# TensorE's order in the second stage written by a driver over bursts, head pairs in one burst, row sums on POOL

## The chip, the cores and the metric

The kernel runs on one core of one Trainium2 chip. The metric is the device time of one execution in microseconds; it is the time of that core. The core's engines are TensorE (PE in the profile), VectorE (DVE), ScalarE (ACT), GpSimd (POOL) and SyncE (SP); each runs its own list of instructions in the order in which the program fixes it, and they meet at semaphores.

## What is computed

One layer of an encoder for two request groups: a prompt group (one stream of 2048 frames) and a sample group (eight streams, 16 frames each, with 4096 past rows). All tensors are float32. Each frame of 1024 features goes through one combined input projection, three parallel groups of heads, and one output projection; a LayerNorm closes the layer. Cut to what matters here:

```python
def _layer(x, w_in, ..., w_out, ln_g, ln_b, hg_state, mem_k, mem_v, ...):
    hq, hf, hv, hgate, fq, fk, fv, fgate, flogf, mq, mgate = _split_in(x @ w_in)
    ...
    o_h, S = _hgrn2(hg_state, q, k, v, log_f)        # gated linear recurrence, 4 heads of 128
    o_f = _fox_prompt(fq, fk, fv, logf)              # attention with decay, 4 heads of 64
    o_m = _cross(mq, mem_k, mem_v)                   # attention to 256 memory rows, 4 heads of 64
    mix = concat(rmsnorm(o_h) * silu(hgate), o_f * silu(fgate), o_m * silu(mgate))
    return layernorm(ALPHA * x + mix @ w_out)
```

## The kernel before, in words

The first stage (up to 1006.65 us) does the input projection, the sample group's attention over its cache and the prompt's first two FoX blocks, and writes what the heads need to DRAM. Products that must keep float32 precision are made of three products of split operands (`xh*wh`, `xh*wl`, `xl*wh`).

The second stage (from 1006.65 us on) is the change's place. The prompt is cut into 16 tiles of 128 frames. For each tile `t` there are three pieces:

- `cross(t)` (from L1143): scores of four heads against the 256 memory rows, in both PSUM banks `f`; a maximum (L1158, VectorE), four exponentials (L1161, ScalarE), transposes, eight values products `h<-cPT,mvt`, a gate.
- `hgrn_tile(t)` (L679): q and k are multiplied by decays level by level (`update`, L708 to L710, VectorE), and after each level TensorE makes a few small products of 32 columns (`L<-hQ,hK`, `h<-hQ,hK`). Then `A`, the state's products, a norm (L823), four transposes (L826), the gate (L828), and `emit_mix`: a cast to `mixHh` (L675, ScalarE) and the rest `mixHl` (L676, VectorE).
- `out_tile(t)` (L1188): two halves of 24 products `o` of the mixes with `woh` and `wol`, the residual (L1207), statistics (L1208) and the LayerNorm passes L1224 and L1225 on VectorE; the tile goes out.

Beside them runs `fox(n)` (L956) for the blocks n = 2 and 3 of 512 queries. For each of two pairs of heads it loads q (`fq1`, `fq2`, two buffers each) and then, for each 128 keys, k and v; it makes the scores of both heads (two products a head, in the banks `f`), their exponentials `fP` (L1003, ScalarE, four buffers), one values product for each head, 64 columns wide, into two halves of the bank `pv` (a float32 product counts as two records), and it adds `fP` to the row sums `facc` (L976, VectorE). q and k come by DMAs that POOL issues (L962 to L965, L989, L991).

The order of the work: `run` (L1229) calls the tiles and FoX in turn by weights; `ahead` (L1237) gives their instructions priorities (`P_CROSS` and `P_HGRN` 1000, `P_FOX` 100), and a scheduler then sets the order of each engine from its own estimates. `load_w_out` (L1105) loads the output weights in eight pieces and splits each half on ScalarE (L1118) and VectorE (L1119), between the steps of tile 0. PSUM's eight banks are `f` twice, `pv`, `h` twice, `L`, and `o` twice.

Of the kernel before, what the change touches and what calls it, by code (L numbers as in the profile page):

```python
# [21 lines left out]
B_FP = 4  # L22
B_O, B_H = 2, 2
FOX_EXTRA = 5
KW, B_WR = 4, 1
FOX_END = 70
P_X = 400
P_CROSS, P_HGRN, P_FOX = [1000, 1000, 100]
# [58 lines left out]
def kernel(  # L87
# [591 lines left out]
    def hgrn_tile(t, hb, psh, psl, hstate, emit_mix, bufs):  # L679
# [10 lines left out]
        V = tl([128, 512], "hV", 1)  # L690
        G = tl([128, 4, 128], "hG", 1)
# [6 lines left out]
        yield  # L698
        L = psl()
        P = F.rearrange("p h t -> p (h t)")  # L700

        def update(b, P):
            n = 512 // (2 * b)
            Pv = P.rearrange("p (n two) -> p n two", two=2)
            q = Q[:, 0].rearrange("p h (n two b) -> p (h n) two b", two=2, b=b)[:, :, 1, :]
            k = K.rearrange("p h (n two b) -> p (h n) two b", two=2, b=b)[:, :, 0, :]
            Pn = tl([128, n], f"P{2 * b}", bufs if b > 2 else 1)
# [9 lines left out]
        yield  # L717
        slot = 2
        M = None
        for b in (2, 4, 8) if smp else (2, 4, 8, 16):  # L720
            P = update(b // 2, P)
            if slot == 4:
                M = psh()
# [6 lines left out]
            yield  # L730
        n2 = slot - 4
        T = tl([128, 768], "hT", 1).rearrange("p (h s t) -> p h s t", h=4, s=6)[:, :, 0:slot, :]
        DVE.tensor_tensor(out=T[:, :, 0:4, :], in0=L, in1=lm3[:, 0:4, :].unsqueeze(1).to_broadcast([128, 4, 4, 32]),
                          op=ALU.mult)
        DVE.tensor_tensor(out=T[:, :, 4:slot, :], in0=M[:, :, 0 : 32 * n2].rearrange("p h (s t) -> p h s t", t=32),
                          in1=lm3[:, 4:slot, :].unsqueeze(1).to_broadcast([128, 4, n2, 32]), op=ALU.mult)
        C = tl([128, 4, 32], "hC", 1)
        DVE.tensor_reduce(out=C, in_=T.rearrange("p h s t -> p h t s"), axis=AX.X, op=ALU.add)
        A = tl([128, 4, 128], "hA", 1)
        DVE.tensor_tensor(out=A.rearrange("p h (i t) -> p h i t", t=32), in0=C.unsqueeze(2).to_broadcast([128, 4, 4, 32]),  # L740
                          in1=bm3.unsqueeze(1).to_broadcast([128, 4, 4, 32]), op=ALU.mult)
        if not smp:
            P = update(16, P)
            for h in range(4):
# [4 lines left out]
            yield  # L749
            P = update(32, P)  # L750
            for h in range(4):
                mm(M[0:64, h, 64:128], K[:, h, 0:64], Q[:, 0, h, 64:128])
            ACT.copy(A[0:64, :, 64:128], M[0:64, :, 64:128])
            ACT.copy(A[0:32, :, 32:64], M[64:96, :, 64:96])
            ACT.copy(A[64:96, :, 96:128], M[96:128, :, 64:96])
            P = update(64, P)
        else:
            P = update(8, P)
        yield
# [3 lines left out]
        o = psh()  # L763
        if not smp:
            kT = tl([128, 768], "hT", 1)[:, 0:512].rearrange("p (h t) -> p h t", h=4)
            ACT.copy(kT, kp)
            S = hstate["S"]
# [11 lines left out]
            hstate["S"] = S2  # L779
            if t == 15:  # L780
                SP.dma_start(p_state, S2)
        else:
            P3 = P.rearrange("p (h b) -> p h b", b=8)
# [31 lines left out]
        yield  # L815
# [7 lines left out]
        DVE.tensor_tensor(out=on, in0=o, in1=ss.unsqueeze(2).to_broadcast([128, 4, 128]), op=ALU.mult)  # L823
        tp = psh()
# [5 lines left out]
        yield  # L830

    def sample_hgrn(stack):
# [12 lines left out]
        yield from hgrn_tile("s", hs, ptr, lambda: pp.tile([128, 512], F32, name="pj", tag="pj", bufs=B_PJ).rearrange("p (h s t) -> p h s t", h=4, s=4), {},  # L845
# [110 lines left out]
    def fox(n):  # L956
        T0 = 512 * n
        c0 = T0 if n < 2 else T0 + 128
        for pr in range(2):
            hs = slice(2 * pr, 2 * pr + 2)  # L960
            q1 = fp.tile([68, 2, 512], F32R, name="fq1", bufs=2)
            POOL.dma_start(q1[0:64], s_qq[0:64, hs, T0 : T0 + 512])  # L962
            POOL.dma_start(q1[64:68], s_m[:, n, pr])
            q2 = fp.tile([128, 2, 512], F32R, name="fq2", bufs=2)
# [3 lines left out]
            todo = []  # L968

            def values(V, st, t0, PT, first, last):  # L970
# [3 lines left out]
                if not first:  # L974
                    for hh in range(2):
                        DVE.tensor_tensor(out=acc[hh][:, t0:], in0=acc[hh][:, t0:], in1=PT[hh][:, t0:], op=ALU.add)  # L976

            for c in range(n + 1):
# [3 lines left out]
                for st in range(4):  # L982
# [10 lines left out]
                    if todo:  # L993
                        todo.pop(0)()
# [10 lines left out]
                    todo.append(lambda V=V, st=st, t0=t0, PT=PT, first=first, last=last: values(V, st, t0, PT, first, last))  # L1005
                    yield
            while todo:
                todo.pop(0)()
            yield
# [13 lines left out]
            yield  # L1023

    def fox_steps(n):
        return 2 * (4 * (n + 1) + 2)
# [24 lines left out]
    SAMPLE_STEPS = DECODE_STEPS + 9  # L1051
# [75 lines left out]
    hstate = {"S": Sp}  # L1127
# [5 lines left out]
    def psl():  # L1133
        return pb.tile([128, 4, 4, 32], F32, name="L", tag="L", bufs=1)

# [7 lines left out]
    def cross(t):  # L1143
# [7 lines left out]
        l = ob.tile([128, 4], F32, name="cl")  # L1151
        pss = [ptf().rearrange("p (c s) -> p c s", c=2) for _ in range(2)]
# [13 lines left out]
        yield  # L1166
        PT = ob.tile([128, 8, 128], F32, name="cPT", bufs=1)
        for half in range(2):
# [4 lines left out]
            ACT.copy(PT[:, half * 4 : half * 4 + 4, :], pt)  # L1173
        o = psh()[:, 0:2, :]
# [11 lines left out]
        yield  # L1186

    def out_tile(t):  # L1188
# [14 lines left out]
        for half in range(2):  # L1203
            c = slice(512 * half, 512 * half + 512)
            ps = ptile("o", B_O)
            project(ps, lambda k: lhs(0, k), lambda k: lhs(1, k), lambda k: woh[:, k, c], lambda k: wol[:, k, c])
            DVE.scalar_tensor_tensor(out=y[:, c], in0=y[:, c], scalar=ALPHA, in1=ps, op0=ALU.mult, op1=ALU.add)  # L1207
            DVE.bn_stats(bs[:, half, :], y[:, c])  # L1208
            yield
# [17 lines left out]
        yield  # L1227

    def run(*streams):  # L1229
        live = [[g, 0, n] for g, n in streams]  # L1230
        while live:
            s = min(live, key=lambda e: (e[1] + 1) / e[2])
            if next(s[0], "end") == "end":
                live.remove(s)
            s[1] += 1

    def ahead(gen, offset):  # L1237
        while True:
            with tc.high_priority(offset=offset):
                r = next(gen, "end")  # L1240
            if r == "end":
                return
            yield

    def tiles():
        wo = load_w_out()
        next(wo)
        for t in range(16):
            for gen, offset in ((cross(t), P_CROSS), (hgrn_tile(t, hb, psh, psl, hstate, emit_mix, 2), P_HGRN)):
                for _ in ahead(gen, offset):  # L1250
                    if t == 0:
                        next(wo, None)
                        next(wo, None)
                    yield
            if t == 0:
                finish(wo)
                yield from out_tile("s")
            yield from out_tile(t)

# [4 lines left out]
    run((tiles(), 16 * 14 + 3), (ahead(fox_gen, P_FOX), (sum(fox_steps(n) for n in range(4)) - EARLY_STEPS) * 100 / FOX_END))  # L1264
# [72 lines left out]
```

## Time and profile before

| | |
|---|---|
| median of three runs | 1597.71 us (1595.32 to 1601.28) |
| profiled execution, its own time | 1597.58 us |
| its span | 1595.8 us |
| first stage, second stage | 1006.65 us, 589.15 us |
| mean granted TensorE clock | 0.985 |
| TensorE, VectorE, ScalarE, POOL busy | 1512.4, 794.4, 481.7, 168.7 us |

The span reaches from the first to the last instruction; 1.8 us of the execution's time lie around it. Busy time of TensorE counts a matmul's record; records overlap by some 0.1 us, so the time that one holds the engine is read from its start to the start of the next. A granted clock of 1.00 is 2.4 GHz, 0.50 is 1.2 GHz. In the timelines `x2` counts adjacent records of one kind, and what stands in brackets is the idle time ahead and the engine and line that ended it.

### The profile page before, as it was taken

How to read it: one execution, taken by the hardware profiler on the slowest of the kernel's cores; microseconds unless marked ns; L12 is line 12 of the kernel's file. 1: busy time of each engine (PE TensorE's matmuls, PEld its weight loads, DVE VectorE, ACT ScalarE, POOL GpSimd, SP SyncE). 2: the span in 40 equal slices, each digit the busy share in tenths (PEclk: the TensorE clock that was granted, in tenths of full speed). 3: DMA queues.
4: the chain of work that ended last, by engine and by line, in shares of the span. 5: the costliest groups of instructions: out<-in, count | busy, mean ns of one | idle time of the engine just before them, and what ended most of it. 6: DMA issues, size and time to landing. Idle time of an engine off the chain costs nothing.

```text
span 1595.8 us, 29721 instructions
## 1 busy us (share of the span) xinstructions
PE 1512.4 (95%) x12119; PEld 1183.6 (74%) x12119; DVE 794.4 (50%) x1630; ACT 481.7 (30%) x1088; POOL 168.7 (11%) x219
## 2 busy tenths in 40 slices
PE   6999999999999989889899999889999999999998
PEld 6999998986986778678887876456566566667776
DVE  4522332221343245555575223477766666668776
ACT  4323322112132311121111333444344333334341
POOL 0610000000001110000010222310111111100000
PEclk9999999999999999999999999999999999999999
DMA  7645459568669864866353675963443343322231
GB/s 245 211 134 170 135 187 293 186 209 260 218 228 277 271 195 145 227 195 189 88 149 127 155 143 119 221 174 91 130 114 97 88 110 97 91 74 87 94 100 60
DMA packets 219527, 254.71 MB, mean 160 GB/s; under 512 B 40190, under 2 KB 165310, under 8 KB 219392
## 3 DMA queue, kind: packets, MB, share of 16 engines
q1 hardware_dynamic: 165984, 217.32, 43.4%
q0 software_dynamic: 53408, 35.51, 11.2%
q8 instruction: 95, 1.56, 0.4%
q14 instruction: 40, 0.33, 0.1%
HBM read 199.55 MB, written 53.12 MB: 158 GB/s over the span
## 4 chain that ended last, share of the span: by engine, by line
PE 71%; DMA 15%; DVE 6%; issue 4%; ACT 3%; SPq 1%; POOL 0%; DVEq 0%; ACTq 0%; POOLq 0%
PE pj L119 32%; PE o L119 11%; PE pv L119 6%; PE h L119 6%; PE f L119 6%; DMA wraw<-in_w_feat_dram 4%; DMA rb<-s_r 2%; PE ds L119 2%; PE dv L119 2%; DMA fP<-s_fg 2%; PE L L119 1%; PE tr L119 1%; DMA xr<-in_x_feat_dram 1%; PE h L1172 1%; DVE wlo L259 1%
## 5 line engine op out<-in xcount | busy, mean ns | idle before, releaser
L119 PE MATMUL pj<-xh,whi 128*128 128x384 f32 (+1 forms) x1056 | 360.9, 342 | 2.8 <-DVE fmx L917 2.7
L119 PE MATMUL pj<-xh,wlo 128*128 128x384 f32 (+1 forms) x1056 | 350.2, 332 | 0.2 <-DVE wlo L259 0.2
L119 PE MATMUL pj<-xl,whi 128*128 128x384 f32 (+1 forms) x1056 | 349.3, 331 | 0.0
L119 PEld LDWEIGHTS pj<-xh,whi 128*128 128x128 f32 x1056 | 201.0, 190 | 22.3 <-issue 15.1
L119 PEld LDWEIGHTS pj<-xl,whi 128*128 128x128 f32 x1056 | 200.8, 190 | 7.4 <-issue 3.6
L119 PEld LDWEIGHTS pj<-xh,wlo 128*128 128x128 f32 x1056 | 200.2, 190 | 3.8 <-issue 3.1
L304 ACT ACTIVATE e<-pj 128x384 f32<-128x384 f32 (+1 forms) x96 | 45.3, 473 | 361.9 <-PE pj L119 324.8
L917 DVE TENSOR_REDUCE fmx<-pj 128x1 f32<-128x512 f32 (+3 forms) x160 | 96.7, 609 | 76.0 <-PE pj L119 74.3
L119 PE MATMUL pj<-whi,xh 128*128 128x256 f32 (+1 forms) x408 | 122.1, 300 | 12.3 <-ACT whi L258 8.7
L259 DVE TENSOR_TENSOR wlo<-wraw,whi 128x1024 fp32r<-128x1024 f32 (+1 forms) x60 | 75.4, 1256 | 115.2 <-ACT whi L258 115.0
L976 DVE TENSOR_TENSOR facc<-facc,fP 128x512 f32<-128x512 f32 (+3 forms) x144 | 83.7, 597 | 72.9 <-ACT fP L1003 72.6
L1003 ACT ACTIVATE fP<-f 128x512 f32<-128x512 f32 (+3 forms) x144 | 73.0, 526 | 153.8 <-PE f L119 146.1
L119 PE MATMUL pj<-whi,xl 128*128 128x256 f32 (+1 forms) x408 | 116.6, 286 | 3.0 <-DVE xl L239 3.0
L119 PE MATMUL pj<-wlo,xh 128*128 128x256 f32 (+1 forms) x408 | 116.3, 285 | 0.5 <-DVE wlo L259 0.5
L119 PE MATMUL pv<-fP,fV 128*64 128x512 f32 (+3 forms) x288 | 105.3, 565 | 5.8 <-ACT fP L1003 5.5
L119 PE MATMUL f<-fq,fk 68*128 68x512 f32 (+5 forms) x320 | 101.2, 407 | 3.4 <-issue 2.0
L119 PEld LDWEIGHTS pj<-whi,xh 128*128 128x128 f32 x408 | 78.5, 193 | 28.5 <-issue 13.1
L119 PEld LDWEIGHTS f<-fq,fk 68*128 68x128 f32 (+1 forms) x320 | 54.5, 195 | 59.0 <-issue 48.6
L258 ACT CAST whi<-wraw 128x1024 fp32r<-128x1024 f32 (+1 forms) x60 | 62.9, 1048 | 101.4 <-DMA wraw<-in_w_feat_dram 95.0
L119 PE MATMUL pj<-fk1m,fq1m 66*128 66x512 f32 (+3 forms) x160 | 64.7, 406 | 23.4 <-DMA fq1m<-s_qq 13.4
L989 POOL DMA_DIRECT2D fk<-s_kk x40 | 39.9, 998 | 398.4 <-PE f L119 393.1
L119 PEld LDWEIGHTS pj<-whi,xl 128*128 128x128 f32 x408 | 78.4, 192 | 4.9 <-DVE xl L239 4.0
(313 smaller groups left out, 2459.2 us busy)
## 6 DMA issues: line engine op xcount, KB each, us to landing
kv<-in_cache_fox_k_dram SPq DMA_DIRECT2D x64, 512.0 KB
kv<-in_cache_fox_v_dram SPq DMA_DIRECT2D x64, 512.0 KB
wraw<-in_w_feat_dram SPq DMA_DIRECT2D x56, 512.0 KB
fk<-s_kk POOLq DMA_DIRECT2D x40, 256.0 KB, 4.5
xr<-in_x_feat_dram SPq DMA_DIRECT2D x34, 256.0 KB
rb<-s_r SPq DMA_DIRECT2D x32, 256.0 KB
y<-in_x_prompt_dram SPq DMA_DIRECT2D x16, 512.0 KB
out_dram<-y SPq DMA_DIRECT2D x16, 512.0 KB
```

Source lines behind the costliest of these rows:

```text
L119: PE.matmul(out, lhsT=lhsT, rhs=rhs, start=start, stop=stop)
L258: pin(ACT.copy(hi[:, r, :w], raw[:, :, :w]))
L259: pin(DVE.tensor_tensor(out=lo[:, r, :w], in0=raw[:, :, :w], in1=hi[:, r, :w].bitcast(F32), op=ALU.subtract))
L304: ACT.activation(e, ps, AF.Sigmoid)
L917: DVE.tensor_reduce(out=mx[:, hh, tt, c : c + 1], in_=ps, axis=AX.X, op=ALU.max)
L976: DVE.tensor_tensor(out=acc[hh][:, t0:], in0=acc[hh][:, t0:], in1=PT[hh][:, t0:], op=ALU.add)
L989: POOL.dma_start(k1, s_kk[64:132, hs, cs])
L1003: ACT.activation(pT[:, t0:], ps[:, t0:], AF.Exp)
L1172: PE.transpose(pt[:, j, :], Pr[:, i // 2, (i % 2) * 128 : (i % 2) * 128 + 128], ident)
```

## The change

1. **Order by a driver.** `run`, `ahead`, `tiles` and the priorities go. `hgrn_tile`, `cross`, `fox` and `out_tile` now yield ahead of each burst of TensorE's work: the tile width of the burst, its estimated duration, a delay from the end of the burst before it, and, where needed, a gate. `drive` holds five streams (even hgrn tiles, odd ones, cross, FoX, out), keeps a clock of its own, prefers a burst of the shape that stands, and takes them in the order hgrn, cross, out, FoX, or with FoX ahead of out while FoX is behind `FOX_US`. TensorE's instructions stay in the order written. `have["H"]` is set once a tile's last hgrn burst is placed.
2. **Both heads of a values product** stand in one burst, after a yield of their own; scores, values and sums of FoX are steps of their own, and `FOX_EXTRA` goes from 5 to 6 such finer steps.
3. **POOL.** The adds to `facc` move from VectorE to POOL. The second LayerNorm pass of each tile but the last becomes a scaling on ScalarE and an add of `lnb` on POOL.
4. **Buffers.** `fP` 4 to 5; `o` 2 banks to 1, and a bank `M` for hgrn's later levels; `hV`, `hG` and `P2` two buffers, `hkT` a tile of its own; `fq1` and `fq2` 2 to 1.
5. **hgrn.** The first four slots of `T` are multiplied while the later levels are made, `A` is made in `within` ahead of the last level; the state's products have a gate on the tile before.
6. **w_out** is loaded and split as a whole ahead of the driver.

```diff
-B_FP = 4
-B_O, B_H = 2, 2
-FOX_EXTRA = 5
+B_FP = 5
+B_O, B_H = 1, 2
+FOX_EXTRA = 6
-P_CROSS, P_HGRN, P_FOX = [1000, 1000, 100]
+FOX_US, FOX_BY = 100.0, 400.0
...
-        yield
+        yield 32, 0.6, 4.0, lambda: hstate["L"]
+        hstate["L"] = False
         L = psl()
...
+        yield 128, 0.45, 5.0
         tp = psh()
         for h in range(4):
             PE.transpose(tp[:, h, :], on[:, h, :], ident)
...
-            q1 = fp.tile([68, 2, 512], F32R, name="fq1", bufs=2)
+            q1 = fp.tile([68, 2, 512], F32R, name="fq1", bufs=1)
...
-            q2 = fp.tile([128, 2, 512], F32R, name="fq2", bufs=2)
+            q2 = fp.tile([128, 2, 512], F32R, name="fq2", bufs=1)
...
-                        DVE.tensor_tensor(out=acc[hh][:, t0:], in0=acc[hh][:, t0:], in1=PT[hh][:, t0:], op=ALU.add)
+                        POOL.tensor_tensor(out=acc[hh][:, t0:], in0=acc[hh][:, t0:], in1=PT[hh][:, t0:], op=ALU.add)
...
-                    if todo:
-                        todo.pop(0)()
+                    size = (512 - t0) / 512
+                    yield 128, 0.95 * size + 0.1 * (c == n), 3.0 if first else 0.3
...
-                    todo.append(lambda V=V, st=st, t0=t0, PT=PT, first=first, last=last: values(V, st, t0, PT, first, last))
-                    yield
+                    yield 64, 0.95 * size, 1.8
+                    values(V, st, t0, PT, first, last)
...
+        yield 64.5, 1.3, 3.0
         pss = [ptf().rearrange("p (c s) -> p c s", c=2) for _ in range(2)]
...
-            ps = ptile("o", B_O)
-            project(ps, lambda k: lhs(0, k), lambda k: lhs(1, k), lambda k: woh[:, k, c], lambda k: wol[:, k, c])
+            for k in range(8):
+                if k % 2 == 0:
+                    yield 128, 1.4, 0.0 if k or B_O > 1 else 1.5
+                if k == 0:
+                    ps = ptile("o", B_O)
+                mm(ps, lhs(0, k), woh[:, k, c], start=(k == 0), stop=False)
...
-            DVE.scalar_tensor_tensor(out=y, in0=y, scalar=rs[:, 0:1], in1=lnb, op0=ALU.mult, op1=ALU.add)
+            ACT.activation(y, y, AF.Copy, scale=rs[:, 0:1])
+            POOL.tensor_tensor(out=y, in0=y, in1=lnb, op=ALU.add)
...
+    def hgrn_tiles(first):
+        for t in range(first, 16, 2):
+            busy[first] = t
+            yield from hgrn_tile(t, hb, psh, psl, hstate, emit_mix, 2, psm)
+            have["H"] = t + 1
...
+    def out_ready():
+        t = need["O"]
+        return t == "s" or min(have["H"], have["C"]) > t and fox_done[0] > t // 4
...
+            can = [s for s in (h, g, x, f, o) if s.live and s.after()]
+            now = [s for s in can if s.ready <= clock]
+            behind = f.done < FOX_US * min(1.0, clock / FOX_BY)
+            hs = [h, g] if busy[0] < busy[1] else [g, h]
+            order = hs + ([x, f, o] if behind else [x, o, f])
+            best = None
+            if shape != 128:
+                best = next((s for s in order if s in now and s.next[0] == shape), None)
+            if best is None:
+                best = next((s for s in order if s in now), None)
...
-    run((tiles(), 16 * 14 + 3), (ahead(fox_gen, P_FOX), (sum(fox_steps(n) for n in range(4)) - EARLY_STEPS) * 100 / FOX_END))
+    finish(load_w_out())
+    with tc.manual_schedule(engines={PE.engine}):
+        drive()
```

How TensorE's rows move, at two places. In a row stand the line, the operation, the output and the operands, the shape, and how many alike follow each other. `pv<-fP,fV` is a values product of one head, `L<-hQ,hK` a small product of hgrn, `f<-fq,fk` a FoX score, `o` an output product. TensorE in the second stage before, among the first FoX steps:

```order
L119 MATMUL L<-hQ,hK 32x64 x16
L119 MATMUL pv<-fP,fV 64x512
L119 MATMUL f<-fq_10243,fk_10682 128x512
L119 MATMUL f<-fq_10246,fk_10684 128x512
L119 MATMUL pv<-fP,fV 64x512
L119 MATMUL L<-hQ,hK 32x32 x16
L119 MATMUL pv<-fP,fV 64x512
```

And in the change, where a FoX score follows the cross scores `f<-mkT,cqg`, and further down a values product:

```order
L118 MATMUL L<-hQ,hK 32x64 x16
L118 MATMUL f<-mkT,cqg 128x256 x4
L118 MATMUL f<-fq_10339,fk_10349 128x512
L118 MATMUL f<-fq_10342,fk_10351 128x512
L118 MATMUL f<-fq_10339,fk_10349 128x512
L118 MATMUL f<-fq_10342,fk_10351 128x512
L118 MATMUL L<-hQ,hK 32x32 x16
```

```order
L1188 MATMUL h<-cb,cP 128x128 x8
L118 MATMUL M<-hQ,hK 32x32 x16
L118 MATMUL pv<-fP,fV 64x512 x2
L118 MATMUL o<-woh,mixF_8640 128x512
L118 MATMUL o<-wol,mixF_8640 128x512
L118 MATMUL o<-woh,mixF_8641 128x512
```

The heads of a pair, apart before, stand together (`x2`), and the scores of FoX follow those of cross at once, in the same two banks. The second place is the end of an hgrn tile, whose last burst are the transposes `h<-cb,hon`. Before:

```order
L119 MATMUL f<-mkT,cqg 128x256 x4
L119 MATMUL o<-woh,mixHh 128x512
L119 MATMUL o<-wol,mixHh 128x512
L119 MATMUL o<-woh,mixHl 128x512
L119 MATMUL o<-woh,mixHh 128x512
L826 MATMUL h<-cb,hon 128x128 x4
L119 MATMUL o<-wol,mixHh 128x512
L119 MATMUL o<-woh,mixHl 128x512
L119 MATMUL o<-woh,mixF_8630 128x512
```

In the change:

```order
L118 MATMUL pv<-fP,fV 64x512 x2
L118 MATMUL L<-hQ,hK 32x32 x16
L118 MATMUL f<-fq_11535,fk_12159 128x512
L118 MATMUL f<-fq_11538,fk_12161 128x512
L118 MATMUL f<-fq_11535,fk_12159 128x512
L118 MATMUL f<-fq_11538,fk_12161 128x512
L841 MATMUL h<-cb,hon 128x128 x4
L118 MATMUL o<-woh,mixHh 128x512
L118 MATMUL o<-wol,mixHh 128x512
L118 MATMUL o<-woh,mixHl 128x512
```

Before, the `o` products around the transposes are those of the tile before, and more of them follow; in the change the first `o` product of the same tile stands right behind its transposes.

## Rows read from the trace of the kernel before

**Rows 1.** The page: busy time of each engine, and its share of the span.
```profile
PE 1512.4 (95%) x12119; PEld 1183.6 (74%) x12119; DVE 794.4 (50%) x1630; ACT 481.7 (30%) x1088; POOL 168.7 (11%) x219
```

**Rows 2.** Windows of the second stage; columns: busy us of each engine, granted clock, DMA share, GB/s.
```profile
1007.00:1588.00 581.00, 564.43 (x5280) 365.25 (x5278) 404.97 (x873) 228.12 (x655) 51.90 (x63) 0.99 0.41 109
1014.50:1017.90 3.40, 3.40 (x7) 1.34 (x6) 2.72 (x6) 0.21 (x1) 0.00 (x0) 0.50 1.52 229
1062.30:1065.70 3.40, 3.40 (x39) 2.24 (x38) 2.63 (x6) 1.14 (x2) 2.58 (x4) 0.50 0.71 158
```

**Rows 3.** Waits of TensorE, 1000 to 1600 us: line, releaser, us in total, times, longest.
```profile
PE pv L119 <- ACT fP L1003: 3.6, 1, 3.6
```

**Rows 4.** Timeline of TensorE in the second stage: start, duration, line, what.
```profile
1014.28 1.60 PE L119 MATMUL pv<-fP,fV 128*64 128x512 f32 x2 [3.60 <-ACT fP L1003]
...
1222.66 1.07 PE L119 MATMUL pv<-fP,fV 128*64 128x512 f32 x2
1223.66 0.50 PE L119 MATMUL o<-woh,mixMh 128*128 128x512 f32 x1
...
1234.70 0.43 PE L119 MATMUL h<-cPT,mvt 128*64 128x128 f32 x2
1235.06 0.25 PE L119 MATMUL h<-hQ,hK 128*32 128x32 f32 x2
1235.24 0.43 PE L119 MATMUL h<-cPT,mvt 128*64 128x128 f32 x2
...
1237.41 1.08 PE L119 MATMUL pv<-fP,fV 128*64 128x512 f32 x4
1238.42 0.74 PE L119 MATMUL f<-fq,fk 68*128 68x512 f32 x2
```

**Rows 5.** The same timeline, around a burst 32 columns wide.
```profile
1213.09 0.40 PE L119 MATMUL o<-woh,mixHl 128*128 128x512 f32 x1
1213.33 0.39 PE L119 MATMUL o<-woh,mixF 128*128 128x512 f32 x1
...
1214.03 0.50 PE L119 MATMUL o<-wol,mixF 128*128 128x512 f32 x1
1214.37 0.62 PE L119 MATMUL o<-woh,mixF 128*128 128x512 f32 x2
```

**Rows 6.** Timeline of all engines at the end of the last hgrn tile.
```profile
1570.85 0.60 PE L826 MATMUL h<-cb,hon 128*128 128x128 f32 x4
...
1572.21 0.62 ACT L675 CAST mixHh<-hon 128x512 fp32r<-128x512 f32 x1 [2.25 <-DVE hon L828]
...
1572.87 0.69 DVE L676 TENSOR_TENSOR mixHl<-hon,mixHh 128x512 fp32r<-128x512 f32 x1
```

**Rows 7.** Timeline of all engines behind the cross scores of one tile.
```profile
1299.79 1.14 PE L119 MATMUL f<-mkT,cqg 64*128 64x256 f32 x8
...
1301.91 1.28 DVE L1225 SCALAR_TENSOR_TENSOR y<-y,brs,lnb 128x1024 f32<-128x1024 f32 x1
...
1303.11 1.28 DVE L1158 TENSOR_REDUCE cmx<-f 128x2 f32<-128x512 f32 x2
...
1304.90 1.08 PE L119 MATMUL f<-facc,cb 128*64 128x512 f32 x4 [1.08 <-ACT cP L1161]
```

**Rows 8.** DMA issues of the second stage: tile, queue, count, KB, median us to landing.
```profile
fq<-s_qq POOLq DMA_DIRECT2D x2, 512.0 KB, 9.3
```

**Rows 9.** Lines of VectorE, 1007 to 1588 us: busy us, mean ns, idle before.
```profile
L976 DVE TENSOR_TENSOR facc<-facc,fP 128x512 f32<-128x512 f32 (+3 forms) x104 | 63.7, 623 | 23.6 <-ACT fP L1003 23.3
...
L1119 DVE TENSOR_TENSOR wol<-y,woh 128x512 fp32r<-128x512 f32 x16 | 10.6, 685 | 4.9 <-ACT woh L1118 4.9
```

**Rows 10.** Timelines of POOL (first two) and VectorE (third) in the first stage.
```profile
38.15 1.89 POOL L474 TENSOR_TENSOR cbb<-cba 128x1024 f32<-128x1024 f32 x1 [36.35 <-DMA cba<-in_cache_fox_logf_dram]
...
45.36 2.73 POOL L474 TENSOR_TENSOR cba<-cbb 128x1024 f32<-128x1024 f32 x1
...
54.63 2.95 DVE L259 TENSOR_TENSOR wlo<-wraw,whi 128x1024 fp32r<-128x1024 f32 x1
```

More of the change, by code (lines that the diff above doesn't have):

```diff
@@ L755, in hgrn_tile @@
             ACT.copy(A[64:96, :, 96:128], M[96:128, :, 64:96])
-            P = update(64, P)
+            hstate["M"] = True
         else:
             P = update(8, P)
-        yield
+            A = within()
+        yield 128, 0.45, 2.5
         kp = psh()
@@ L844, in sample_hgrn @@
         yield
-        yield from hgrn_tile("s", hs, ptr, lambda: pp.tile([128, 512], F32, name="pj", tag="pj", bufs=B_PJ).rearrange("p (h s t) -> p h s t", h=4, s=4), {},
+        yield from hgrn_tile("s", hs, ptr, lambda: pp.tile([128, 512], F32, name="pj", tag="pj", bufs=B_PJ).rearrange("p (h s t) -> p h s t", h=4, s=4), {"L": True, "M": True},
                            lambda t, mf: out(mf, 0, 4), 1)
@@ L1237, in ahead, with __init__, after, step @@
[L1237 to L1247, printed above, removed]
-        for t in range(16):
[L1249 to L1257, printed above, removed]
-            yield from out_tile(t)
+    class Stream:
+        def __init__(self, gen, after=lambda: True):
+            self.gen, self.limit, self.ready, self.done, self.live = gen, after, 0.0, 0.0, True
+            self.step()
+        def after(self):
+            return self.limit() and (len(self.next) < 4 or self.next[3]())
+        def step(self):
+            self.next = next(self.gen, None)
+            self.live = self.next is not None
@@ new lines, in hgrn_tiles, with crosses, outs @@
+    def hgrn_tiles(first):
[3 more added lines that the diff above has]
+            have["H"] = t + 1
+    busy = [0, 1]
+    def crosses():
+        for t in range(16):
+            yield from cross(t)
+            have["C"] = t + 1
+    def outs():
+        for t in ["s"] + list(range(16)):
+            need["O"] = t
+            yield from out_tile(t)
+            have["O"] = 0 if t == "s" else t + 1
@@ new lines, with drive @@
+    have = {"H": 0, "C": 0, "O": 0}
+    need = {"O": "s"}
+    made = {}
+    def out_ready():
+        t = need["O"]
+        return t == "s" or min(have["H"], have["C"]) > t and fox_done[0] > t // 4
+    def drive():
+        h = Stream(hgrn_tiles(0), lambda: busy[0] < have["O"] + 2)
+        g = Stream(hgrn_tiles(1), lambda: busy[1] < have["O"] + 2)
+        x = Stream(crosses(), lambda: have["C"] < have["O"] + 2)
+        f = Stream(fox_gen)
+        o = Stream(outs(), out_ready)
+        clock, shape = 0.0, 128
+        while any(s.live for s in (h, g, x, f, o)):
+            can = [s for s in (h, g, x, f, o) if s.live and s.after()]
[8 more added lines that the diff above has]
+                best = next((s for s in order if s in now), None)
+            if best is None:
+                best = min(can, key=lambda s: s.ready)
+                clock = max(clock, best.ready)
+            kind, us = best.next[:2]
+            clock += us + (0.25 if kind != shape else 0.0)
+            shape = kind
+            best.done += us
+            best.step()
+            if best.live:
+                best.ready = clock + best.next[2]
```

88 lines of the change are left out of this document (45 added, 43 removed).

## Prediction, before the result was known

> **What bounds the kernel now.** I read the busy shares first. TensorE works 95% of the span, VectorE 50%, GpSimd (POOL) 11% [rows 1]. The changed parts run almost wholly in the second stage, so I cut the windows there: from 1007 to 1588 us TensorE is busy 564.4 of 581 us, VectorE 405, POOL 52 [rows 2]. The waits view of TensorE shows what ended the other 16.6 us: the largest single wait is 3.6 us for the first exponential of a FoX block [rows 3]; none recurs at scale. So the stage is bound by how long TensorE's slots are, and its order, made by a scheduler, already hides nearly all waits. A change can win only by shorter slots, and it loses whatever waits it opens. The windows hold a second thing: four stretches of 3.4 us have a granted clock of 0.50, the lower of its two levels (1.2 instead of 2.4 GHz), and the first of them comes right behind that longest wait, which ends at 1014.28 [rows 2 to 4]. A stretch at half clock costs about 1.7 us of work. Later, without such waits, the clock holds.
>
> **Slots that get shorter.** A values product of one head that stands alone holds TensorE 1.00 us (1222.66 to 1223.66); two heads side by side take 1.01 (1237.41 to 1238.42) [rows 4]. In the order of before, 27 pairs of the 512-wide shape are apart, about eight narrower ones too; the changed order has all pairs side by side. That is 27 x 0.99 = 27 us, plus 4 for the narrow ones (up to 0.75 each at 384, in proportion below): **-31 us**.
>
> The cross products (values of the cross branch, `h<-cPT,mvt`) stand alone 67 times of 128 before, at 0.36 us (1234.70 to 1235.06) [rows 4]; the change has all eight of a tile in one burst. At 0.25 of a 512-wide pair, a pair of 128-wide ones takes 0.27, so one costs some 0.14 and 67 x 0.22 = **-15 us**; if a product in a burst costs 0.19 it is 11. The FoX sums go into one burst in the same manner, by the same prices at most 2 us: **-2 us**.
>
> Shape changes of TensorE's tile (128, 64 or 32 wide): the orders show 515 before and 288 after, 227 fewer, of which some 67 lie in the cross price already. A burst of two records 32 wide held TensorE 0.18 us [rows 4]; the first `o` product behind a 32-wide burst takes 0.34, between its like 0.24 [rows 5]. In and out again is thus up to 0.28, some 0.15 a change: 160 x 0.15 = **-24 us** (half of that if most of the 0.18 is the work). Together **-72 us**.
>
> **Waits that the fixed order opens.** *Out behind its own mix.* After a tile's last hgrn transposes four steps run: VectorE's gate product, ScalarE's cast to `mixHh`, VectorE's remainder `mixHl`. The transposes at 1570.85 end at 1571.45; `mixHh` ends at 1572.83, `mixHl` at 1573.56: 1.4 and 2.1 us with both engines free [rows 6]. Before, `o` products of that tile come over 20 us of TensorE rows later in ten of sixteen tiles. The driver sets `have["H"]` as soon as the last burst is placed, and the new order has less than 3 us of work in between at 13 of 16 tiles, none at seven. VectorE is busy 405 of 581 us [rows 2], so its queue often stands ahead: 13 x 1.4 = 18 at least, 13 x 4.2 = 55 at most, and I take 2.7 each: **+35 us**.
>
> *Fox scores behind cross scores.* Cross scores fill both `f` banks and free them only when the maximum (VectorE) and four exponentials (ScalarE) have read them. The row shows it: scores at 1299.79, next writer of `f` at 1304.90, 5.1 us, with a LayerNorm pass ahead of the maximum on VectorE [rows 7]. In the new order a FoX score follows at once or within 4 us at 13 of 16 tiles. The chain is 3 us without the LayerNorm pass and 5 with it; less cover it is 1.2 to 4.5, eleven or so times: 13 to 55, taken **+36 us**. First values behind their exponentials, with bursts of scores right ahead, add **+5** (0 to 10).
>
> *Single buffers of q.* `fq1` and `fq2` have one buffer, so a new pair of heads can load only after the last scores of the old one. Landing takes 9.3 us [rows 8] plus 2 of issue; the new order leaves 2 to 14 us of other rows at the seven switches. 11.3 less that cover sums to 26; the smaller transfers land sooner: **+15** (0 to 26).
>
> *The tail.* After the last values product the new order holds only 210 `o` products and the last hgrn tiles, 84 us of slots where before had over 150. VectorE's work of a tile, without adds and weight split, is (405-64-11)/16 = 20.6 us [rows 2, 9]; 4.4 tiles are left, 91 us, in a chain that TensorE must follow level by level. **+30** (11 to 50). *The start:* all of w_out is loaded and split before the driver instead of between the steps of tile 0. VectorE's 16 halves are 10.6 us, ScalarE's as much [rows 9], and hgrn's first steps stand behind them: **+12** (0 to 25).
>
> **POOL.** 112 row-sum adds of the stage leave VectorE (104 of 63.7 us, the rest rebuilt like them) [rows 9], sixteen LayerNorm passes leave too. That alone is worth little, since VectorE ends few waits. No 512-wide add on POOL is in the trace; a 1024-wide one took 1.89 us alone and 2.73 while VectorE ran two-operand work, and VectorE's 1024-wide split took 2.95 in that stretch, where twice a half of 0.685 [rows 9] would be 1.37 [rows 10]. So an add is 0.95 to 1.4 us, and the two hold each other up; hgrn's steps on VectorE, which TensorE waits for, are of that kind. Net of relief **+10** (-20 to +40). The Trainium skill, "SBUF — State Buffer", section "SBUF: two separate sides", says that VectorE with two SBUF inputs and GpSimd take their shared ports as an exclusive lock; the trace agrees (1.89 against 2.73). The skill's "GPSIMD Engine Reference", section 4.1, advises VectorE for elementwise adds, at a measured ratio of 1.96; by that, as an estimate, an add would be 1.34 us and the sum would stay.
>
> **Clock.** Before, waits of 1.3 to 3.6 us came ahead of each of the four stretches at 0.50. The change opens some 35 of that size; if half bring such a stretch, 18 x 1.7 = **+30** (7 to 50).
>
> The rest (finer FoX steps, one more step taken early, earlier `A`, the `M` bank, one `o` bank) moves work between covered places; I cost it at nothing, hidden by TensorE's slots. With one `o` bank each half waits for VectorE's read (0.7), which the driver covers with 1.5 us of delay; bare it would be 33 x 0.8 = 26, inside the range.
>
> **The sum.** -72 + 35 + 36 + 5 + 15 + 30 + 12 + 10 + 30 = +101, less the 16.6 us of old waits that these replace: +84. The profiled execution took 1597.6 us (span 1595.8 and 1.8 around it), the median of three is 1597.7: **1682 us**.
>
> **Rivals.**
> *The gain holds (faster).* The driver counts on delays of 2.2 to 7 us behind each burst and puts other streams there. If waits stay at their lower ends (18 + 13 + 11 + 7, the rest nothing, less 17) they are 32 us and the time is 1598 - 72 + 32 = 1558. For it: five streams to choose from, VectorE relieved. Against it: rows with no cover in the order itself, the `o` stream without any delay. It decides if the mix chain and the f banks cost under 1.5 us a tile each. Chance 0.13.
> *Waits just eat the gain:* about 1600, between these; a measurement of this kernel can tell some 0.5% (8 us) from no change. Chance 0.11, half of it within that.
> *POOL sets the pace (slower still).* POOL does adds in the queue that issues `fk`. At 1.4 us four adds ahead of an `fk` pair are 5.6, with 1.7 of issue and 4.5 of landing 11.8, against some 9 of cover: 26 pairs x 2.5 = 65 more, 1747. For it: the 2.73 row. Against it: POOL's sum is only 112 x 1.4 + 15 x 2.7 + 52 = 250 of 580 us. It decides from about 1.3 us an add. Chance 0.12.
> *The pairs don't run together:* nearly excluded, since the order has them side by side and the row of such a pair shows 1.01.
>
> **Numbers.** Forecast 0.64 (its range alone 1615 to 1740), the others as above. Faster by over 0.5%: 0.13 and a little of the second rival, 0.15; within: 0.06; slower: 0.79. Range 1592 to 1758: it leaves out the faster case and the far end of POOL's.
>
> **What would show it.** In the new profile: values products as pairs at 1.01 and TensorE's busy slots 70 us less at full clock; waits of `o` for `mixHh`/`mixHl`, of `f` for `cP`, of 1 to 4 us, some ten times each; slices with PEclk under 9 in the second stage; VectorE's `facc` line gone, and POOL's at 0.95 to 1.4. It is wrong if TensorE's idle time in the second stage is under 70 us, or if its busy time does not fall.

## The result, and the profile after

The changed kernel takes 1696.3 us (median of four, 1692.3 to 1697.8), before 1598.6 us: a ratio of 1.061 (95% interval 1.058 to 1.064). It is slower by 98 us. The profiled execution took 1696.47 us, its span is 1694.7 us. The page's busy shares and slices after; they answer to [rows 1]:

```profile
PE 1499.9 (89%) x12119; PEld 1196.8 (71%) x12119; DVE 776.2 (46%) x1470; ACT 493.8 (29%) x1103; POOL 364.3 (21%) x379
...
PE   7999999999999998999998987777788888888776
...
POOL 1610000000011100001003763343324343431100
PEclk9999999999999999999999996888898899889778
```

TensorE is busy 12.5 us less in all, but 89% of a longer span; POOL's busy time has more than doubled. In the first 24 slices the shares and the clock are much as before. From there on, in the second stage, TensorE is at 7 and 8 tenths (6 in the last slice), and its granted clock is under 9 tenths in 12 of the 16 slices; before it was 9 in every slice. The window of the second stage of the kernel before, to its end (columns as in [rows 2]):

```profile
1007.00:1595.80 588.80, 564.65 (x5280) 365.25 (x5278) 409.30 (x880) 228.62 (x657) 51.90 (x63) 0.98 0.40 108
```
And of after: the stage, its first 43 us, and what lies behind the last values product:

```profile
1007.00:1694.70 687.70, 549.02 (x5288) 374.59 (x5284) 411.61 (x760) 242.21 (x675) 216.83 (x192) 0.86 0.34 95
1007.00:1050.00 43.00, 25.66 (x183) 11.49 (x179) 21.41 (x43) 17.77 (x38) 18.30 (x21) 0.68 0.98 258
1558.00:1694.70 136.70, 102.52 (x998) 77.39 (x997) 77.12 (x155) 38.75 (x122) 9.62 (x4) 0.82 0.17 57
```

Busy time counts a product at half clock about double: the record of an `o` product takes 0.79 us at 1178.98 below, where the granted clock was 0.50, and 0.40 in [rows 5]. So I cut the stage into windows of 2 us and took, in each, busy time times (1 - granted clock) as lost to the clock; what is left of busy time is the work at full clock. Of the stage, in us:

| kernel | length | idle | lost to the clock | work at full clock |
|---|---|---|---|---|
| before | 588.8 | 24.1 | 6.1 | 558.5 |
| changed | 687.7 | 138.7 | 69.9 | 479.1 |
| difference | +98.9 | +114.6 | +63.8 | -79.5 |

The work became shorter by 79 us, and waits and clock took 178 back. Two lines of the work, the values products of FoX and of cross, by form (columns as in [rows 9]); before, these took 74.9 and 39.9 us, in the lines shown with the last experiment:

```profile
L118 PE MATMUL pv<-fP,fV 128*64 128x512 f32 x160 | 51.6, 684 | 0.4 <-ACT fP L1015 0.4
...
L118 PE MATMUL h<-cPT,mvt 128*64 128x128 f32 x256 | 19.1, 295 | 0.0
```

The waits of TensorE in the second stage (line and releaser, total, times, longest), which answer to [rows 3]:

```profile
PE f L118 <- ACT cP L1177: 31.3, 12, 8.2
PE o L118 <- ACT mixHh L674: 25.7, 11, 3.4
PE L L118 <- DVE hK L709: 12.4, 6, 4.6
PE o L118 <- DVE mixHl L675: 11.2, 7, 2.5
PE h L774 <- DVE hK L709: 10.5, 5, 3.6
PE M L118 <- DVE hT L740: 7.1, 5, 2.0
...
PE f L118 <- DMA fq<-s_m: 3.0, 1, 3.0
...
PE f L118 <- DMA fq<-s_qq: 2.2, 1, 2.2
```

One wait for the f banks is the clearest picture of the change (timeline of all engines, in order of time):

```profile
1121.56 1.13 PE L118 MATMUL f<-mkT,cqg 64*128 64x256 f32 x8
...
1124.90 0.69 DVE L1029 TENSOR_TENSOR fP<-fP 128x512 f32<-128x512 f32 x1 [2.75 <-DMA fP<-s_fg]
...
1127.45 1.28 DVE L1245 SCALAR_TENSOR_TENSOR y<-y,bmv,lng 128x1024 f32<-128x1024 f32 x1
...
1128.64 1.28 DVE L1174 TENSOR_REDUCE cmx<-f 128x2 f32<-128x512 f32 x2
...
1129.87 0.46 ACT L1177 ACTIVATE cP<-f,cmx 128x256 f32<-128x256 f32 x1
1130.06 2.35 POOL L1247 TENSOR_TENSOR y<-y,lnb 128x1024 f32<-128x1024 f32 x1 [11.57 <-ACT y L1246]
...
1130.35 2.35 DVE L695 TENSOR_SCALAR hK<-hF 128x512 f32<-128x512 f32 x1 [0.43 <-DMA hF<-s_f]
...
1130.93 2.13 PE L118 MATMUL f<-fq,fk 68*128 68x512 f32 x4 [8.24 <-ACT cP L1177]
```

The cross scores start at 1121.56 and end 1.13 us later. The maximum on VectorE comes only at 1128.64: ahead of it in VectorE's queue lies a step of FoX's gate (L1029), whose operand is still being loaded, so that VectorE itself is idle for 2.75 us; then come statistics and a LayerNorm pass. FoX's scores, next in TensorE's fixed order, wait 8.24 us, and the clock is at 0.50 when they start: four records take 2.13 us. Beside it, POOL's add of `lnb` holds VectorE: `hK<-hF` takes 2.35 us, where before 16 such took 0.448 on average. Six of the sixteen in the change run into such an add, and each of the six ends 0.28 or 0.29 us behind it; the other ten took 0.41 to 0.65 us. The second recurring wait, behind the mix of the tile itself (TensorE alone):

```profile
1170.75 0.66 PE L841 MATMUL h<-cb,hon 128*128 128x128 f32 x4
...
1175.74 0.80 PE L118 MATMUL o<-woh,mixHh 128*128 128x512 f32 x1 [2.94 <-ACT mixHh L674]
...
1178.98 0.79 PE L118 MATMUL o<-woh,mixHl 128*128 128x512 f32 x1 [2.01 <-DVE mixHl L675]
```

Lines of POOL in the second stage (columns as in [rows 9]):

```profile
L988 POOL TENSOR_TENSOR facc<-facc,fP 128x512 f32<-128x512 f32 (+3 forms) x106 | 123.0, 1179 | 144.8 <-ACT fP L1015 134.4 <-ACT hss L835 9.8
L1247 POOL TENSOR_TENSOR y<-y,lnb 128x1024 f32<-128x1024 f32 x16 | 38.3, 2394 | 172.9 <-ACT y L1246 163.7 <-ACT hss L835 9.2
```
And of VectorE, first the step `hQ` before, then two lines of the change:

```profile
L708 DVE TENSOR_TENSOR hQ<-hQ,P 128x256 f32<-128x256 f32 x96 | 40.4, 420 | 28.7 <-PE h L119 21.0 <-PE L L119 7.5
```
```profile
L708 DVE TENSOR_TENSOR hQ<-hQ,P 128x256 f32<-128x256 f32 x96 | 58.7, 612 | 85.8 <-PE M L118 69.4 <-PE L L118 16.3
...
L745 DVE TENSOR_TENSOR hA<-hC,cb 128x512 f32<-128x512 f32 x16 | 19.3, 1208 | 0.1
```

An add to the row sums took 1.18 us over its four widths; the 80 that are 512 wide took 1.32 us each, within the 0.95 to 1.4 of the prediction and close to its other estimate of 1.34. On VectorE, hgrn's `hQ` steps went from 420 ns a piece to 612, `hA` from 683 to 1208.

### The profile page after: what moved, and what is told of

It reads as the page before. It is cut to its first block, busy times and chain, and to the rows that moved or that the text cites. A ratio compares the mean times of both kernels' runs of the same rounds, so it can differ in the third digit from the quotient of the medians.

```text
span 1694.7 us, 29843 instructions
## 1 busy us (share of the span) xinstructions
PE 1499.9 (89%) x12119; PEld 1196.8 (71%) x12119; DVE 776.2 (46%) x1470; ACT 493.8 (29%) x1103; POOL 364.3 (21%) x379
## 4 chain that ended last, share of the span: by engine, by line
PE 61%; DMA 15%; DVE 13%; issue 5%; ACT 4%; SPq 1%; POOL 1%; DVEq 0%; ACTq 0%; POOLq 0%
PE pj L118 31%; PE o L118 11%; PE f L118 4%; DMA wraw<-in_w_feat_dram 4%; PE pv L118 4%; DMA rb<-s_r 2%; PE h L118 2%; DMA hF<-s_f 2%; PE ds L118 2%; PE dv L118 2%; DMA xr<-in_x_feat_dram 1%; DVE hQ L708 1%; PE M L118 1%; DMA fq1m<-s_qq 1%; DVE P L710 1%
## 5 line engine op out<-in xcount | busy, mean ns | idle before, releaser
L988 POOL TENSOR_TENSOR facc<-facc,fP 128x512 f32<-128x512 f32 (+3 forms) x144 | 159.3, 1127 | 145.2 <-ACT fP L1015 134.4
L118 PE MATMUL f<-fq,fk 68*128 68x512 f32 (+4 forms) x320 | 105.5, 448 | 42.9 <-ACT cP L1177 29.1
L118 PEld LDWEIGHTS f<-fq,fk 68*128 68x128 f32 (+1 forms) x320 | 59.8, 219 | 71.2 <-ACT cP L1177 34.4
L708 DVE TENSOR_TENSOR hQ<-hQ,P 128x256 f32<-128x256 f32 x99 | 60.0, 606 | 85.8 <-PE M L118 69.4
L118 PE MATMUL o<-woh,mixHh 128*128 128x512 f32 x144 | 72.9, 507 | 27.9 <-ACT mixHh L674 25.7
L118 PE MATMUL pv<-fP,fV 128*64 128x512 f32 (+3 forms) x288 | 81.4, 586 | 0.6 <-ACT fP L1015 0.4
```

The costliest lines, as they stand in the source:

```text
L118: PE.matmul(out, lhsT=lhsT, rhs=rhs, start=start, stop=stop)
L988: POOL.tensor_tensor(out=acc[hh][:, t0:], in0=acc[hh][:, t0:], in1=PT[hh][:, t0:], op=ALU.add)
```

## The experiments

Two theories. **A:** each wait counts for itself, so covering it wins its length and its share of the clock. **B:** the streams' chains through VectorE and ScalarE set the pace, and a covered wait turns up at the next place. And beside both: how much of it is POOL's, and how much the fixed order's. The table at the end gives each run's ratio to the kernel before as it ran beside that run (medians of 1594.3 to 1598.6 us); the stage's three parts are cut as above, from the profiled execution.

### The waits covered, one and both

```diff
             best.done += us
+            if best is x and kind == 64.5:
+                f.ready = max(f.ready, clock + BANK_US)
+            ended = have["H"]
             best.step()
             if best.live:
                 best.ready = clock + best.next[2]
+            if have["H"] != ended:
+                o.ready = max(o.ready, clock + MIX_US)
```

The first run has only the lines on `ended` with `MIX_US = 4.0`:

> The changed kernel with one edit: the driver offers a tile's out products only 4 us of its clock after that tile's last hgrn burst. Theory A, each wait counts for itself: the waits of the out products for mixHh and mixHl (25.7 and 11.2 us in the changed kernel) go to under 10 us, and with them half as much that the lower clock takes, so 1696 falls to 1640 to 1665. Theory B, the chains of the streams through VectorE and ScalarE set the pace and a covered wait turns up at the next place: the waits for the mixes fall as well, but others grow by about as much, and the time stays within 10 us of 1696.

The second has only the lines on `x`, with `BANK_US = 5.0`:

> The changed kernel with one edit: after a tile's cross scores the driver holds FoX back for 5 us of its clock. Theory A, each wait counts for itself: the waits of f for cP (31.3 us) go to under 10 us, and the time falls to 1645 to 1670. Theory B, a covered wait turns up at the next place: f's waits for cP fall, others (out behind its mix, hgrn behind VectorE) grow, and the time stays within 10 us of 1696.

The third has both:

> The changed kernel with the edits of the two runs before together. Theory A: the two gains add up, 1590 to 1640. Theory B: what is covered turns up elsewhere, less than 35 us are won, 1660 to 1696; TensorE's idle time in the second stage stays over 100 us of the 139.

Measured: 1667.8, 1683.1 and 1653.4 us: 29, 13 and 43 us less than the change. That is between the theories' ranges in all three. The waits of the first run:

```profile
PE f L119 <- ACT cP L1178: 33.1, 20, 5.1
PE L L119 <- DVE hK L710: 26.3, 16, 6.0
PE o L119 <- DVE y L1230: 9.8, 11, 2.0
```
And those of the third:

```profile
PE L L120 <- DVE hK L711: 31.5, 21, 2.7
PE h L776 <- DVE hK L711: 13.7, 5, 4.6
PE M L120 <- DVE hK L711: 10.9, 8, 2.6
```

Of the 36.9 us of waits for the mixes 1.4 are left in the first run, of the 31.3 for `cP` 0.4 in the third; and TensorE's waits for hgrn's steps on VectorE grew, for `L` from 12.4 to 26.3 and 31.5 us, for `hK` in all from 23 to 33 and 56. In the first run the waits of `o` for `y`, the residual that reads the one bank `o`, grew as well, from 2.2 to 9.8 us. Idle time fell by 18 of the 37 us covered, and in the third run by 29 of 68. So each theory holds half: about half of a covered wait turns up elsewhere, in the third run mostly (33 of 39 us) where TensorE waits for `hK`. The two gains add up (29 + 13 and 43).

### Work put into a wait: the clock

```diff
                 if k == 0:
                     ps = ptile("o", B_O)
+                    if half == 0 and t != "s":
+                        for _ in range(10):
+                            mm(ps, lhs(0, 4), woh[:, 4, c])
```

> The changed kernel with ten products more at the start of each tile's out products, into the bank that the first real product then overwrites, of operands that are long ready: 160 products of 0.24 us, 38 us of work, most of it where TensorE waits for mixHh. It is a measure of the clock: TensorE is busy in place of idle and nothing comes earlier. If the stretches at the lower clock come from the waits, TensorE's idle time falls by 20 to 37 us, the time lost to the clock by some 10 to 20 of its 70, and the time stays within 15 us of 1696 or falls below it. If the clock does not hang on these waits, its loss stays at 70 and the time is 1700 to 1735.

Measured: 1711.5 us (1702.7 to 1719.8); the profiled execution, the fastest of the four, has a span of 1700.9 us. The work at full clock rose by the 38 us put in (517 against 479), idle time fell by 18, the loss to the clock from 70 to 56. So 38 us of work that speeds up nothing cost 6 us of the profiled span and 15 of the median. The median lies at the far edge of what was expected if the clock hangs on the waits, and inside the range for the other case; idle time, too, fell by a little less than the 20 us expected. What decides is the clock's loss, which did not stay at 70: all four executions have a mean granted clock of 0.942 to 0.948, the four of the change 0.934 to 0.936. So it is shown for this part that the clock's loss hangs on the waits: 14 us for 18 us of idle time, beside the change's own 64 for 115.

### The row sums back on VectorE

```diff
-                        POOL.tensor_tensor(out=acc[hh][:, t0:], in0=acc[hh][:, t0:], in1=PT[hh][:, t0:], op=ALU.add)
+                        DVE.tensor_tensor(out=acc[hh][:, t0:], in0=acc[hh][:, t0:], in1=PT[hh][:, t0:], op=ALU.add)
```

In the kernel with both delays:

> The kernel of the run with both delays, and the adds to the row sums back on VectorE. In the changed kernel VectorE's hgrn steps hQ took 612 ns a piece in the second stage, before 420, and TensorE waits for them. Theory: POOL's adds hold VectorE up, so hQ falls back to under 470 ns, TensorE's waits for hK fall from 56 to under 40 us, and 1653 falls to 1625 to 1645, although VectorE gets 64 us of adds more. Rival: VectorE is simply behind in its queue; the adds put the same time back and 1653 stays or rises to 1670.

Measured: 1625.2 us, 28 less than 1653.4. VectorE's lines:

```profile
L990 DVE TENSOR_TENSOR facc<-facc,fP 128x512 f32<-128x512 f32 (+3 forms) x108 | 64.1, 615 | 33.9 <-ACT fP L1017 33.5
...
L710 DVE TENSOR_TENSOR hQ<-hQ,P 128x256 f32<-128x256 f32 x96 | 44.6, 465 | 25.3 <-PE M L120 23.0 <-PE L L120 2.1
```
And TensorE's waits:

```profile
PE L L120 <- DVE hK L711: 30.2, 20, 4.7
...
PE h L776 <- DVE hK L711: 6.9, 4, 3.8
PE M L120 <- DVE hK L711: 5.0, 6, 1.4
```

VectorE has 64 us of adds more to do, and its `hQ` steps are faster: 465 ns, where in the run with both delays they took 693. POOL's adds hurt because they held VectorE up, not because POOL was late (no wait of TensorE names a POOL step): the rival, an equal exchange, is out. The waits for `hK` fell from 56 to 42 us, a little less than expected (under 40).

### POOL alone, in the kernel before

```diff
-                        DVE.tensor_tensor(out=acc[hh][:, t0:], in0=acc[hh][:, t0:], in1=PT[hh][:, t0:], op=ALU.add)
+                        POOL.tensor_tensor(out=acc[hh][:, t0:], in0=acc[hh][:, t0:], in1=PT[hh][:, t0:], op=ALU.add)
```

> The kernel before with the adds to the row sums on POOL, nothing else of the change. Theory: TensorE's order is the scheduler's and hides waits, VectorE's hgrn steps get longer (over 500 ns) as POOL's adds hold them up, and the time stays within 8 us of 1598, since VectorE ends few waits there. Rival: the exclusion alone opens waits behind hK, and 1610 to 1640 comes out.

Measured: 1640.6 us, 1.027 (1.023 to 1.031), just above the rival's range. My theory was wrong here and the rival right: this scheduler's order does not hide VectorE's longer steps. The waits, first the one line for `hK` in the kernel before:

```profile
PE h L119 <- DVE hK L709: 2.4, 5, 1.5
```
```profile
PE h L119 <- DVE hK L709: 14.6, 15, 3.7
PE L L119 <- DVE hK L709: 7.0, 4, 2.9
PE h L762 <- DVE hK L709: 6.3, 4, 2.4
```
And VectorE's lines, first `hK` in the kernel before:

```profile
L709 DVE TENSOR_TENSOR hK<-hK,P 128x256 f32<-128x256 f32 x96 | 40.0, 417 | 0.0
```
```profile
L709 DVE TENSOR_TENSOR hK<-hK,P 128x256 f32<-128x256 f32 x96 | 64.7, 674 | 0.0
L708 DVE TENSOR_TENSOR hQ<-hQ,P 128x256 f32<-128x256 f32 x96 | 49.3, 513 | 31.6 <-PE L L119 19.2 <-PE h L119 12.1
```

The 2.4 us of waits for `hK` before became 28, with 18 us more lost to the clock; `hK` steps take 674 ns where before 417. (The profiled execution, 1647.9 us, is the slowest of four. The scheduler also laid TensorE's rows otherwise, 7 us of work more.) The same adds put back in the change alone, by the edit of the section before:

> The changed kernel with the adds to the row sums back on VectorE, nothing else. Theory: POOL's exclusion costs by itself, about as much as in the run with the delays (28 us) or in the kernel before (44 us): 1650 to 1675, VectorE's hQ steps under 470 ns. Rival: while the order's own waits are there, a faster hgrn chain only waits longer elsewhere, and the time stays within 10 us of 1696.

Measured: 1674.4 us, 22 less than the change (18 by the two ratios to the kernel before), in the range expected; the `hQ` steps take 482 ns, a little over the 470 named, and TensorE's waits for `hK` and `hT` fell from 30 to 16 us. In the profiled execution, the slowest of four, the input projection's last product ends at 1024.1 us, in the change at 1006.9; what follows it is 32 us shorter than in the change. Whether the edit made the first stage longer is not shown.

### The order left free

```diff
-    with tc.manual_schedule(engines={PE.engine}):
-        drive()
+    drive()
```

> The changed kernel with TensorE's order left to the scheduler, which takes the driver's program only as a priority; buffers, POOL's adds and everything else stay. Theory: the fixed order itself opens the waits for the mixes and the f banks (68 us), so these fall to under 25 us and 1696 falls to 1625 to 1660, no further, since POOL's exclusion (44 us when it was put into the kernel before) is still in it; most pairs stay side by side. Rival: the waits come from buffers and POOL, the order is only where they show, and 1675 to 1700 comes out.

Measured: 1657.0 us, 39 less than the change (35 by the two ratios). The waits for the f banks are 10.2 us, those for the mixes 5.7 in all:

```profile
PE L L118 <- DVE hK L709: 17.9, 11, 3.3
...
PE f L118 <- ACT cP L1177: 10.2, 12, 1.7
...
PE o L118 <- DVE mixHl L675: 4.3, 3, 2.9
```

So the fixed order costs some 40 us: without it idle time is 39 us less and the clock's loss 24 less, while the work is 25 us more, and 44 of 54 pairs still stand together. The 63 us that this run loses against the kernel before remain with a free order. The driver's program still sets its priorities, so that the driver has no part in them is not shown.

### The gain without the driver

```diff
-                for hh in range(2):
-                    r = slice(64 * hh, 64 * hh + 64)
-                    mm(pv[r, t0:], V[:, st, r], PT[hh][:, t0:], start=first, stop=last)
+                with tc.high_priority(offset=5000):
+                    for hh in (1, 0):
+                        r = slice(64 * hh, 64 * hh + 64)
+                        ins = PE.matmul(pv[r, t0:], lhsT=V[:, st, r], rhs=PT[hh][:, t0:], start=first, stop=last)
+                        if hh == 0:
+                            pin(ins)
```

`pin` keeps an instruction behind the one ahead of it on its engine. Head 1 goes first, since its exponential is the later one.

> The kernel before, scheduler and all, with one edit: the two heads of a values product of FoX are kept side by side on TensorE, the second behind the first. This is the one saving of the change without its driver. Theory: 27 pairs of 0.99 us and some narrow ones are saved and no wait is opened, since only a head's product moves by a few us: 1598 falls by 20 to 31 us, to 1567 to 1578. Rival: holding the first head until the second's exponential is there costs what it saves, 1590 to 1605.

The second run does the same with the eight products of cross:

```diff
-        for pr in range(2):
-            for st in range(2):
+        with tc.high_priority(offset=5000):
+            ins = None
+            for pr in range(2):
+                for st in (1, 0):
...
+                        lead = ins is None
+                        ins = PE.matmul(o[64 * hh : 64 * hh + 64, pr, :], lhsT=mvt[:, st, 64 * h : 64 * h + 64],
+                                        rhs=PT[:, 2 * h + st, :], start=(st == 1), stop=(st == 0))
+                        if not lead:
+                            pin(ins)
```

> The run before it, and the eight values products of a tile's cross branch kept side by side in the same manner. Theory: 67 products that stood alone cost 0.22 us less each and shape changes go from 473 to 357, together 15 to 20 us more: 1547 to 1563. Rival: the burst waits for the last transposed probabilities and only moves the time, 1565 to 1580.

Measured: 1578.4 us, 0.987 (0.984 to 0.991), at the upper edge of its range, with six executions between 1567.8 and 1582.9, and 1547.6 us, 0.970 (0.967 to 0.973), at the lower edge. The second stage of the second run:

```profile
1007.00:1545.80 538.80, 506.68 (x5296) 346.40 (x5292) 411.17 (x880) 227.38 (x659) 52.96 (x65) 0.98 0.45 119
```
Its values products by form (line, operands, shape, records; busy us, mean ns; idle ahead):

```profile
L974 PE MATMUL pv<-fP,fV 128*64 128x512 f32 x160 | 44.7, 638 | 2.4 <-ACT fP L1006 2.2
...
L1185 PE MATMUL h<-cPT,mvt 128*64 128x128 f32 x256 | 18.7, 282 | 0.0
```
The same lines of the kernel before:

```profile
L119 PE MATMUL pv<-fP,fV 128*64 128x512 f32 x160 | 74.9, 650 | 3.9 <-ACT fP L1003 3.6
...
L119 PE MATMUL h<-cPT,mvt 128*64 128x128 f32 x256 | 39.9, 292 | 0.0
```

The FoX heads take 44.7 us in place of 74.9, the cross products 18.7 in place of 39.9. Idle time and the clock's loss stay nearly as before (32.1 and 6.9 us against 24.1 and 6.1). This version beats both kernels: 49 us less than before, 149 less than the change.

### All runs

| run | us | ratio to before | idle | clock | work | work, whole span |
|---|---|---|---|---|---|---|
| before | 1598.6 | 1 | 24.1 | 6.1 | 558.5 | 1492.8 |
| the change | 1696.3 | 1.061 | 138.7 | 69.9 | 479.1 | 1415.5 |
| out products later | 1667.8 | 1.045 | 120.6 | 56.6 | 481.5 | 1414.0 |
| FoX later behind cross | 1683.1 | 1.053 | 126.7 | 56.0 | 488.4 | 1424.3 |
| both | 1653.4 | 1.034 | 109.7 | 47.5 | 489.0 | 1422.6 |
| both, row sums on VectorE | 1625.2 | 1.019 | 87.8 | 37.8 | 489.6 | 1418.8 |
| row sums on VectorE alone | 1674.4 | 1.050 | 122.1 | 54.1 | 496.2 | 1413.4 |
| order left free | 1657.0 | 1.037 | 99.4 | 46.2 | 504.0 | 1435.2 |
| work in the wait | 1711.5 | 1.071 | 120.6 | 56.3 | 517.0 | 1454.5 |
| before, POOL alone | 1640.6 | 1.027 | 49.2 | 24.4 | 565.6 | 1500.4 |
| before, pairs | 1578.4 | 0.987 | 28.9 | 9.4 | 521.6 | 1457.0 |
| before, pairs and cross | 1547.6 | 0.970 | 32.1 | 6.9 | 499.8 | 1429.9 |

Idle time, clock and work are those of 1007 us to the end. Where a run's first stage ends later, or some FoX steps lie a little sooner or later around that point, the work moves from one side to the other, by 17 us in the run with the row sums on VectorE alone; the last column, cut in the same way over the whole span, does not have this.

## Why the prediction was right

The sign, and the time in the main (1682 forecast, 1696 measured), came from the mechanism that the prediction named: shorter slots, outweighed by waits and by the clock that they cost. That the fixed order opens these waits is shown for a part of them: leaving it free took 39 of the 115 us of new idle time away, moving the row sums back 17 (22 beside the delays). How much of the rest is due to the buffers, to w_out or to the adds of `lnb` on POOL, no run tells. Step by step:

- **Slots, -72:** -79 measured (-77 over the whole span). The pairs were -31 in the sum; the run with pairs alone shows 37 us less work, in an execution of 1568.7 us, 29 less than the profiled one before; its median is 19 less. The cross products (-15 and -2) are another 22 us of work (27 over the whole span) and 31 of the median. Some 14 to 21 us are left, where the sum had 24 for shape changes; no run takes that rest apart.
- **Out behind its own mix, +35:** 25.7 + 11.2 = 36.9 us of waits. Right in size, but worth only 29 when it was covered (18 of idle time, 13 of the clock), since half of it turned up elsewhere.
- **FoX behind cross scores, +36:** 31.3 us of waits, twelve times, up to 8.2; worth 13 alone. The longest has a part that the prediction did not see, VectorE's 2.75 us behind the load of FoX's gate.
- **First values, +5:** 2.1. **Single buffers of q, +15:** 5.2 in the second stage. Both too large.
- **Tail, +30:** behind the last values product (1557.8 us) TensorE is idle 34.2 of 136.7 us, where before it was 10.7 of 170.8: +23, the mix's waits there included; 11.6 us are waits for `hK`, as put. **Start, +12:** up to 1050 us 17.3 us idle against 7.7, +10. But 5.2 of them are the waits for q above and 4.6 are waits for `cP`; of the cause named, only this shows: casts of w_out on ScalarE (1035.96 and 1037.92) stand ahead of and between those exponentials.
- **POOL, +10:** this term was mis-sized. The prediction's step "Net of relief +10", by which the adds that leave VectorE nearly pay for the two holding each other up, failed: putting them back won 22 and 28 us, moving them alone cost 44. The waits for `hK` and `hT` behind VectorE, 30 us in the change, are where it shows: with the sums back they are 16. The range given (-20 to +40) held the value measured in the change.
- **Clock, +30:** 64, above the range given (7 to 50). The prediction counted 18 stretches of 1.7 us of work, by the four of before, which last 3.4 us. The trace shows 25 stretches at 0.50, and only five of them last 3.4 us; the others last 5.5 to 13.7. They are 195 us of the stage, 70 us of its work lost, 2.8 a stretch. So the length of a stretch was mis-sized more than their number. That is the largest miss of the sum.

That the total came within 14 us is in part luck: the clock cost 34 us more than the sum had, idle time grew by some 12 less (115, the sum had 126 net of the old waits), and the slots saved 7 more.

By the Trainium skill's "SBUF — State Buffer" ("SBUF: two separate sides") the loser of the shared ports waits for the whole instruction: the trace agrees, `hK<-hF` ending 0.3 us behind POOL's add (1132.70 and 1132.41). The ratio of 1.96 that the prediction gave by the Trainium skill's "GPSIMD Engine Reference" stands there in section 3.1; section 4.1 says about twice as slow. Here 512-wide adds took 1.32 us on POOL and 0.684 on VectorE before, a ratio of 1.92.

The rival of held gains fell, since the waits did not stay at their lower ends, and so did the one in which they just eat the gain. POOL as the pace-setter fell as it was put: its condition, some 1.3 us an add, was met by the 512-wide adds, but POOL was busy 217 of 688 us and no wait of TensorE for `fk` came up. It was VectorE that POOL slowed.

What stays open: the 42 us of waits for `hK` that are left with both delays and the sums on VectorE were not taken apart further. The sixteen adds of `lnb` stay on POOL in every run of the changed kernel; with the row sums back, `hK<-hF` still takes 697 ns, and 833 beside the delays, against 448 before, and what that costs was not measured by itself. Two buffers for q in the changed kernel were not tried. Whether a driver with better estimates would beat the pinned version was not tried.

## What to carry to other kernels

Where one engine is busy 97% of a stage and a scheduler hides its waits, take the shorter slots alone: here products pinned side by side brought 49 us, while the change with its order written by hand cost 98. An order written from estimated delays has to name every wait of a shared bank or a freshly cast operand, and a wait there was paid for again in the clock. Work that moves to an idle engine is not free if the engine on the chain gets slower beside it (`hQ` 420 to 612 ns here): price the neighbour's longer steps, not the idle engine's time.

## What was not expected of the hardware

- A VectorE step with a single SBUF operand, `hK<-hF` of 128x512, took 2.35 us beside a POOL add that read SBUF; in the kernel before it took 0.448 on average. In the change 16 of these took 0.897 on average, six of them behind such an add. I had counted only steps with two operands.
- The clock took back over half as much as the waits did: 64 us for 115 us of idle time, with the lower level granted in 195 of 688 us, where before it was 18 of 589. A stretch at the lower level came to 7.8 us on average, up to 13.7, where the first four of before last 3.4.
